# A row softmax: the scheduled kernel rewritten as one critical section with its own semaphores, the exponentials as loops with register addresses

**Chip, cores, metric.** One core of one Trainium2 chip. The metric is the time of one execution in microseconds (us) on the device, measured repeatedly. The profile's span, from the first recorded instruction to the last, is 1.8 us shorter than the measured time in nearly every run here.

## The reference

```python
def reference(x):                       # x: 16 x 1024 x 512 float32
    x_scaled = x / 0.5
    x_max = np.max(x_scaled, axis=-1, keepdims=True)
    exp_x = np.exp(x_scaled - x_max)
    return exp_x / np.sum(exp_x, axis=-1, keepdims=True)
```

That is 16384 rows of 512 numbers; 33.55 MB are read and 33.55 MB written.

## The kernel before

The rows form eight chunks of 128 partitions x 16 rows x 512 (4.19 MB). Six chunk buffers are used in rotation. Chunks are cut into eleven blocks: 4, 4, 8 rows of the first chunk, six whole chunks, 8 and 8 rows of the last. VectorE takes the negated maxima of a block (`shift`), ScalarE the exponentials with their row sums, VectorE the reciprocals and most of the product, and ScalarE one eighth of the product. The queue engine SyncE issues loads, ScalarE stores. Scheduling is manual, but the framework sets the semaphores.

```python
    def shift(i):                                   # VectorE
        ...
        nc.vector.tensor_reduce(negmax[:, 0:b], chunks[c][:, lo:hi, :], axis=AX, op=MAX, negate=True)
        nc.vector.tensor_scalar_mul(biases[i][:, 0:b], negmax[:, 0:b], 2.0)

    def exponentials(i):                            # ScalarE, unrolled
        ...
        for g in range(hi - lo):
            row = chunks[c][:, lo + g, :]
            nc.scalar.activation(out=row, in_=row, func=EXP, bias=biases[i][:, g : g + 1],
                                 scale=2.0, accum_out=sums[i][:, g : g + 1])

    def scale_vector(i):                            # VectorE: reciprocal, then product over 7/8 of the rows
        ...
    def scale_scalar(i):                            # ScalarE: the remaining eighth
        ...
    def store(i):                                   # one store per chunk, on ScalarE's queue
        ...
    shift(0); shift(1); exponentials(0)
    for i in range(n):
        if i + 1 < n:
            exponentials(i + 1)
        scale_vector(i)
        scale_scalar(i)
        if i + 2 < n:
            shift(i + 2)
        store(i)
```

(Cuts are marked with `...`.)

Of the kernel before, what the change touches and what calls it, by code (L numbers as in the profile page):

```python
# [1 line left out]

# [4 lines left out]


@with_exitstack
def kernel(  # L10
    ctx: ExitStack,
    tc: tile.TileContext,
    x: bass.AP,
    out: bass.AP,
):
    nc = tc.nc
    fp32 = mybir.dt.float32
    P = nc.NUM_PARTITIONS
    AX = mybir.AxisListType.X
    EXP = mybir.ActivationFunctionType.Exp  # L20
    COPY = mybir.ActivationFunctionType.Copy
    MAX = mybir.AluOpType.max

    D = x.shape[-1]
    xf = x.flatten_outer_dims()
    of = out.flatten_outer_dims()
    N = xf.shape[0]




    G = 16
    C = N // (P * G)
    assert C * P * G == N
    xr = xf.rearrange("(c p g) d -> c p g d", p=P, g=G)
    outr = of.rearrange("(c p g) d -> c p g d", p=P, g=G)
    WHOLE = [(0, G)]
    LOADS = [[(0, 4), (4, G)]] + [WHOLE] * 7
    BLOCKS = [[(0, 4), (4, 8), (8, G)]] + [WHOLE] * 6 + [[(0, 8), (8, G)]]
    STORES = [WHOLE] * 8  # L40
    BMAX = 16
    BUFS = 6

    data = ctx.enter_context(tc.tile_pool(name="data", bufs=BUFS))
    stats = ctx.enter_context(tc.tile_pool(name="stats", bufs=6))

    ctx.enter_context(tc.manual_schedule())


    warm = stats.tile([P, 1], fp32, name="warm", bufs=1)  # L50
    nc.vector.memset(warm, 0.0)  # L51
    nc.scalar.activation(out=warm, in_=warm, func=EXP)  # L52

    chunks = {}
    blocks = [(c, lo, hi) for c in range(C) for lo, hi in BLOCKS[c]]
    n = len(blocks)
    biases, sums, recips = {}, {}, {}

    def load(c):
        if c < BUFS:  # L60
            chunks[c] = data.tile([P, G, D], fp32, name="xt")
        else:
            chunks[c] = chunks[c - BUFS]
        xt = chunks[c]
        for lo, hi in LOADS[c]:
            nc.sync.dma_start(out=xt[:, lo:hi, :], in_=xr[c][:, lo:hi, :])  # L66

    def shift(i):
        c, lo, hi = blocks[i]
        if c not in chunks:  # L70
            load(c)
        b = hi - lo
        negmax = stats.tile([P, BMAX], fp32, name="negmax")
        nc.vector.tensor_reduce(  # L74
            negmax[:, 0:b], chunks[c][:, lo:hi, :], axis=AX, op=MAX, negate=True
        )
        biases[i] = stats.tile([P, BMAX], fp32, name="bias")
        nc.vector.tensor_scalar_mul(biases[i][:, 0:b], negmax[:, 0:b], 2.0)  # L78

    def exponentials(i):  # L80
        c, lo, hi = blocks[i]
        sums[i] = stats.tile([P, BMAX], fp32, name="sums")
        for g in range(hi - lo):
            row = chunks[c][:, lo + g, :]
            nc.scalar.activation(  # L85
                out=row,
                in_=row,
                func=EXP,
                bias=biases[i][:, g : g + 1],
                scale=2.0,  # L90
                accum_out=sums[i][:, g : g + 1],
            )


    def scale_vector(i):
        c, lo, hi = blocks[i]
        b = hi - lo
        k = b - b // 8
        recips[i] = stats.tile([P, BMAX], fp32, name="recip")
        nc.vector.reciprocal(recips[i][:, 0:b], sums[i][:, 0:b])  # L100
        rows = chunks[c][:, lo : lo + k, :]
        nc.vector.tensor_mul(  # L102
            rows, rows, recips[i][:, 0:k].unsqueeze(2).broadcast_to((P, k, D))
        )

    def scale_scalar(i):
        c, lo, hi = blocks[i]
        b = hi - lo
        for g in range(b - b // 8, b):
            row = chunks[c][:, lo + g, :]  # L110
            nc.scalar.activation(  # L111
                out=row, in_=row, func=COPY, scale=recips[i][:, g : g + 1]
            )

    def store(i):
        c, _, end = blocks[i]
        for lo, hi in STORES[c]:
            if hi == end:
                nc.scalar.dma_start(
                    out=outr[c][:, lo:hi, :], in_=chunks[c][:, lo:hi, :]  # L120
                )

    shift(0)
    shift(1)
    exponentials(0)
# [5 lines that stand above are left out]
        if i + 2 < n:  # L131
            shift(i + 2)
        store(i)


# [1 line left out]
_INS = ['x']  # L137
_OUTS = [((16, 1024, 512), 'float32')]


# [23 lines left out]
```

## Time and profile before

| | kernel before |
|---|---|
| time | 162.44 us median of 4 runs (162.20 to 162.51) |
| span of the profile | 160.57 us |
| transfers | the two data queues are busy 97.7% of the span |
| VectorE / ScalarE busy | 84% / 64% |
| first load issued / last store issued | 0.73 / 147.55 us |
| span's end after the last landing's wait | 0.80 us |

Read it from the bottom of the dependency: the two data queues carry all 67.1 MB and fill the sixteen DMA engines for 97.7% of the span, so their share of busy time decides first. VectorE's 84% comes second, and its place in the chain is what makes it matter. ScalarE is idle for the other 36%, and 41.2 us of that, 26% of the span, ended when a bias came from VectorE. The lines themselves stand in the prediction.

### The profile page before, as it was taken

What the parts mean: (1) busy time and instruction counts of PE and PEld (TensorE: products, weight loads), DVE (VectorE), ACT (ScalarE), POOL (GpSimd) and SP (SyncE); (2) the same over time, 40 slices, a digit from 0 to 9 for tenths busy, and PEclk for the clock granted to TensorE, in tenths of its full rate; (3) what the DMA queues carried; (4) which work ended last, traced back from release to release, by engine and by line L of the source; (5) the groups of instructions that cost most, each with busy time, mean ns of one, the idle gap of its engine ahead of it and who ended that gap; (6) DMA issues with size and microseconds to landing.
All of it is one profiled execution on the core that took longest, in us unless ns stands there. A gap on an engine that the chain in (4) does not pass through costs nothing.

```text
span 160.6 us, 402 instructions
## 1 busy us (share of the span) xinstructions
DVE 134.6 (84%) x45; ACT 102.1 (64%) x273; POOL 0.2 (0%) x4
## 2 busy tenths in 40 slices
DVE  0507999999999999999999999999999999957000
ACT  3071549069979963998199909991899891790000
POOL 0000000000000000000000000000000000000000
DMA  5999999999999999999999999999999999999993
GB/s 182 471 400 506 400 400 498 408 392 484 424 400 384 400 457 449 400 441 465 400 424 473 408 408 492 400 392 498 416 392 490 424 392 457 457 392 449 465 392 139
DMA packets 2450, 67.13 MB, mean 418 GB/s; under 512 B 272, under 2 KB 272, under 8 KB 272
## 3 DMA queue, kind: packets, MB, share of 16 engines
q1 hardware_dynamic: 1296, 33.56, 49.3%
q10 hardware_dynamic: 1152, 33.55, 48.4%
q14 instruction: 2, 0.02, 0.0%
HBM read 33.55 MB, written 33.55 MB: 418 GB/s over the span
## 4 chain that ended last, share of the span: by engine, by line
DVE 80%; DMA 7%; ACT 4%; issue 0%; SPq 0%
DVE negmax L74 42%; DVE xt L102 36%; DMA xt<-in_x_dram 7%; ACT xt L85 4%; DVE bias L78 1%; DVE recip L100 1%; SPq L66 0%
## 5 line engine op out<-in xcount | busy, mean ns | idle before, releaser
L85 ACT ACTIVATE xt<-xt,bias 128x512 f32<-128x512 f32 x128 | 90.4, 708 | 41.7 <-DVE bias L78 41.2
L74 DVE TENSOR_REDUCE negmax<-xt 128x16 f32<-128x8192 f32 (+2 forms) x11 | 69.9, 6352 | 9.5 <-DMA xt<-in_x_dram 9.5
L102 DVE TENSOR_TENSOR xt<-xt,recip 128x7168 f32<-128x7168 f32 (+2 forms) x11 | 62.0, 5637 | 0.4
L85 ACT ACTIVATION_READ_ACCUMULATOR xt<-xt,bias 128x1 f32 x128 | 23.9, 187 | 0.0
L111 ACT ACTIVATE xt<-xt,recip 128x512 f32<-128x512 f32 x15 | 9.9, 706 | 0.0
L100 DVE RECIPROCAL recip<-sums 128x16 f32<-128x16 f32 (+2 forms) x11 | 2.4, 218 | 1.8 <-ACT xt L85 1.8
L78 DVE TENSOR_SCALAR bias<-negmax 128x16 f32<-128x16 f32 (+2 forms) x11 | 1.9, 173 | 0.4
L52 ACT ACT_TABLE_LOAD x1 | 1.3, 1283 | 0.7 <-PEq L148 0.7
L51 DVE MEMSET warm<- 128x1 f32 x1 | 0.1, 59 | 0.8 <-PEq L148 0.8
L52 ACT ACTIVATE warm<-warm 128x1 f32<-128x1 f32 x1 | 0.2, 203 | 0.0
L148 POOL MEMSET const-bfloat16-1.0<- 128x1 bf16 x1 | 0.1, 103 | 0.0
L148 POOL MEMSET const-uint8-127<- 128x1 uint8 x1 | 0.1, 103 | 0.0
L148 POOL MEMSET const-float32-1.0<- 128x1 f32 x1 | 0.1, 100 | 0.0
L148 POOL MEMSET const-float32-0.0<- 128x1 f32 x1 | 0.1, 99 | 0.2 <-issue 0.2
## 6 DMA issues: line engine op xcount, KB each, us to landing
out_dram<-xt ACTq DMA_DIRECT2D x8, 4096.0 KB, 22.8
xt<-in_x_dram SPq DMA_DIRECT2D x7, 4096.0 KB, 30.2
xt<-in_x_dram SPq DMA_DIRECT2D x1, 3072.0 KB, 11.7
xt<-in_x_dram SPq DMA_DIRECT2D x1, 1024.0 KB, 4.9
```

Of the source, the lines that this page charges most:

```text
L51: nc.vector.memset(warm, 0.0)
L52: nc.scalar.activation(out=warm, in_=warm, func=EXP)
L74: nc.vector.tensor_reduce(negmax[:, 0:b], chunks[c][:, lo:hi, :], axis=AX, op=MAX, negate=True)
L78: nc.vector.tensor_scalar_mul(biases[i][:, 0:b], negmax[:, 0:b], 2.0)
L85: nc.scalar.activation(out=row, in_=row, func=EXP, bias=biases[i][:, g : g + 1], scale=2.0, accum_out=sums[i][:, g : g + 1],)
L100: nc.vector.reciprocal(recips[i][:, 0:b], sums[i][:, 0:b])
L102: nc.vector.tensor_mul(rows, rows, recips[i][:, 0:k].unsqueeze(2).broadcast_to((P, k, D)))
L111: nc.scalar.activation(out=row, in_=row, func=COPY, scale=recips[i][:, g : g + 1])
L148: nc = _bacc.Bacc("TRN2", target_bir_lowering=False, num_devices=1)
```

## The change

Its intent: no scheduler bookkeeping, one counting semaphore per engine plus one for each transfer, and a short instruction stream on ScalarE, as a block's exponentials become a loop whose row, bias and sum addresses are computed in registers. (A semaphore is a counter that one engine raises and another waits for; the profile lists what an engine's sequencer does, such as branches, register operations and DMA issues, with a q behind the engine's name, as ACTq, and the engine's own work without it.) What is computed, the order on each engine, the transfers and the six chunk buffers are the same; the small tiles of maxima, biases and sums become one tile of each kind. The diff, cut to its core:

```diff
-    ctx.enter_context(tc.manual_schedule())
+    ctx.enter_context(tc.tile_critical(no_gpsimd_drain=True))
+    vector_done = tc.alloc_semaphore("vector_done")
+    scalar_done = tc.alloc_semaphore("scalar_done")
+    loaded = {(c, hi): tc.alloc_semaphore(...) ...}          # one per load
+    stored = [tc.alloc_semaphore(f"stored_{c}") for c in range(C)]
...
+        vector(lambda: nc.vector.wait_ge(vector_done, done), False)   # between maximum and bias
...
     def exponentials(i):
         c, lo, hi = blocks[i]
-        for g in range(hi - lo):
-            row = chunks[c][:, lo + g, :]
-            nc.scalar.activation(out=row, in_=row, func=EXP, bias=..., accum_out=...)
+        scalar(lambda: nc.scalar.wait_ge(vector_done, need), 0)
+        summed[i] = scalar(lambda: exponential_loop(c, lo, hi), hi - lo)
+    def exponential_loop(c, lo, hi):
+        with nc.scalar.Fori(lo, hi) as g:
+            exponential(c, bass.ds(g, 1)).then_inc(scalar_done, 1)
...
+        scalar(lambda: nc.scalar.wait_ge(vector_done, scaled[i]), 0)  # ahead of a store
+        scalar(lambda: nc.scalar.wait_ge(scalar_done, need), 0)
...
+    for c in range(C - BUFS, C):
+        sync(lambda c=c: nc.sync.wait_ge(stored[c], 16))              # ahead of the section's end
```

## The prediction

The forecast's sum came to 0 + 0 + 0.25 + 0.2 + 0.3 = 0.75 us on 162.41, 163.2 us. What no trace or run of this case shows is cut from the text, with the cuts marked: figures for single steps of the sequencer and for the bandwidth; the terms worked out from them (the sequencer's time for a row of the loop, which was to add 0 us, the time to enter a loop, from which the 0.25 us came, and the cost of waits that are not merged); and the checks that followed from the entry.

> **What bounds the kernel now.** I read the page first: busy shares, the slices, the DMA queues.
>
> ```profile
> DVE 134.6 (84%) x45; ACT 102.1 (64%) x273; POOL 0.2 (0%) x4
> DMA  5999999999999999999999999999999999999993
> q1 hardware_dynamic: 1296, 33.56, 49.3%
> q10 hardware_dynamic: 1152, 33.55, 48.4%
> HBM read 33.55 MB, written 33.55 MB: 418 GB/s over the span
> ```
>
> The two queues together fill 97.7% of the sixteen engines' span. What is missing is 2.3% of 160.6 us, 3.7 us, and the slices put it into the first and the last slice. So the transfers leave no hole anywhere between, and no compute saving can take out more than the two ends hold.
>
> Then the chain of waits and, in the groups, VectorE's own idle time:
>
> ```profile
> by line: DVE negmax L74 41.7%; DVE xt L102 36.2%; DMA xt<-in_x_dram 7.3%; ACT xt L85 3.6%; DVE bias L78 1.1%; DVE recip L100 0.9%; issue 0.4%; SPq L66 0.2%
> ...
> 137.36 0.18 DVE bias L78
> 137.54 0.02 issue
> 137.56 5.76 ACT xt L85 x16
> 143.33 0.02 issue
> 143.35 0.21 DVE recip L100
> 143.56 0.02 issue
> 143.59 3.89 DVE xt L102
> ```
>
> From the second load's landing at 12.86 us VectorE runs without a pause to 147.48, except once: in the last block its reciprocal waits 1.8 us for ScalarE's exponentials. That is the only place where ScalarE lies on the chain. The chain ends 13 us before the span, since the last store is not one of its pieces.
>
> Does that store's issue time matter, with the transfers full? I compared the two lines' times to landing:
>
> ```profile
> DMA to landing us min/median/max: 12.2/22.8/32.4
> ...
> DMA to landing us min/median/max: 4.9/26.3/71.8
> ```
>
> The first answer is for the stores, the second for the loads. The shortest store is the last one: issued at 147.55, 4.19 MB. The shortest load is the first, 1.05 MB into empty queues. [...] So the last store waited for nobody: the store ahead was finished just as its own packets were ready to start. Transfers and VectorE's chain end in a tie. I call the slack of the last store's issue 0 to 0.3 us: earlier gains nothing, later costs the whole delay.
>
> Last, ScalarE's line (exponentials, then the idle time of their first row):
>
> ```profile
> L85 ACT ACTIVATE xt<-xt,bias 128x512 f32<-128x512 f32 x128 | 90.4, 708 | 41.7 <-DVE bias L78 41.2
> L85 ACT ACTIVATION_READ_ACCUMULATOR xt<-xt,bias 128x1 f32 x128 | 23.9, 187 | 0.0
> 79.62 0.72 ACT L85 ACTIVATE xt<-xt,bias 128x512 f32<-128x512 f32 x1 [4.00 <-DVE bias L78]
> ```
>
> The reads of the accumulator overlap the next exponential: in the timeline rows start 0.705 us apart. In a steady block sixteen rows take 63.01 to 74.31, two copies last to 75.63, the store is issued at 75.65 for 0.34 us, and the next block's bias comes 3.6 us later. The block's period is VectorE's: 8.61 + 0.17 + 0.17 + 7.63 and three gaps of 0.02, 16.6 us.
>
> [...] The trace of before has no branch in its body. [...]
>
> **The change part by part.** Loads, stores, sizes, buffers, blocks, and the order of instructions on every engine stay. So do both large VectorE operations (8677 and 7624 ns), hence the 16.6 us period.
>
> *Scheduler's waits replaced by own semaphores.* In the trace a dependent VectorE instruction starts 0.02 us after the one it waits for. There is nothing to gain. I expect the explicit waits to be merged into the instruction behind them, so 0 us. [...]
>
> *Unrolled exponentials become a loop.* 128 pairs of ACTIVATE and accumulator read become eleven loops. ScalarE's engine work is unchanged, 0.705 us a row. New is the sequencer's work per row. My estimate: three addresses (row, bias, sum) need about five register operations, the counter one[...]. Under 0.705 us, so the sequencer runs ahead and rows still start 0.705 us apart. [...]the number of register operations is a guess.
>
> *Entering a loop.* The wait for the bias now stands ahead of a loop[...]; then come a move, a branch and the first row's addresses before the first ACTIVATE[...]. In ten blocks this lies in ScalarE's 3.6 us of waiting and costs nothing. In the last block it goes onto the chain[...]. Less the slack of 0 to 0.3 us: +0.25 us.
>
> *The section's ends.* Entering and leaving a critical section may bring a drain and a barrier more. The existing entry barrier lasts to 0.7 us, and the end takes 0.8 us from the last landing (147.55 + 12.2 = 159.75) to the span's end. I put +0.2 us ahead of the first load, which shifts everything because loads start the chain and the transfers are full, and +0.3 us after the last store.
>
> Sum: 0 + 0 + 0.25 + 0.2 + 0.3 = 0.75 us on 162.41, 163.2 us.
>
> **The rivals.** *The loop is slower than the engine.* Let a row take s in the sequencer. Between 0.705 and about 0.90 us only the last block shows it: eight rows, up to 8 x 0.2 = 1.6 us, total about 164.7. [...] Beyond that ScalarE becomes the bound: at s = 1.1 us each steady block grows by 16 x 0.2 = 3.2 us; with about seven blocks of sixteen rows that is 22 us, about 185. For it: three register addresses per row[...]. [...] I give the first form two chances in ten, the second one in ten.
>
> *Own waits are costlier on VectorE.* [...] For it: VectorE has no slack on its chain. Against it: waits on the instruction itself are what the present 0.02 us gaps look like.
>
> *It gets faster.* For it: fewer instructions, fewer fetches, no scheduler bookkeeping; the first load could go out ahead of the 0.7 us barrier. Against it: the transfers are full from about 2 us to 159 us, so all there is to win is part of that 0.7 us: 161.9 at best. Two per cent, 3.2 us, is not there. In the same way a delay of earlier stores is hidden: the store issued at 133.08 lands 17.0 us later, 7 us more than its bytes need.
>
> **Range and chances.** The central sum is 163.2. Below, a free entry and merged waits give 162.2. Above, the mild form of the slow loop or unmerged waits give 164 to 165.5. Slower by over 2% means above 165.7: the strong loop rival with one chance in ten, and the sum of mild ones with a few more in a hundred. Faster by 2% needs fewer bytes.
>
> **What would show it.** In the changed profile the queues' shares should again add up to 97% or more, with the middle slices full. Product and reduction on VectorE should keep 7624 and 8677 ns, and gaps of 0.02 to 0.1 us between. Starts of exponentials inside a loop should stay 0.705 us apart; if larger, s is read there directly. [...] A first load issued much later than 0.73 us, VectorE waiting for exponentials in every block, or a DMA slice below 9 in the middle would make the prediction wrong.

## The result, and the profile after

The changed kernel takes 163.00 us (median of 4 runs, 162.65 to 163.19) against 162.44 us. The ratio is 1.0035, interval 1.0015 to 1.0055. Ratios here are the mean time of one kernel's fast runs over that of the other's of the same rounds, so not quite the ratio of the medians quoted. It is slightly slower, clear of noise, and well within 2%.

The page of the changed kernel, same lines as in the prediction:

```profile
DVE 134.6 (83%) x45; ACT 102.4 (63%) x273; POOL 0.2 (0%) x4
DMA  4999999999999999999999999999999999999991
q1 hardware_dynamic: 1296, 33.56, 49.1%
q10 hardware_dynamic: 1152, 33.55, 48.2%
```

The queues fill 97.3% of a span that is 0.84 us longer. Multiplied out they are as busy as before (156.9 and 157.1 us), and the middle slices stay full. Only the first and the last digit fell. So I looked for the added time at the two ends.

The start. These are the first seven loads on the queue engine's timeline, start and length; first the kernel before, then the changed one:

```profile
0.73 3.50 SPq L66 DMA_DIRECT2D xt<-in_x_dram  x7
```

```profile
0.94 3.51 SPq L86 DMA_DIRECT2D xt<-in_x_dram  x7
```

The first load goes out 0.21 us later: two more instructions, an empty one of the section's line L56 and a branch, now stand ahead of it on its engine.

The end. Here are instructions of the queue engine, with number, durations in ns (min/median/max), then first and last start in us; first the kernel before:

```profile
L159 SPq DRAIN  x3: 7/7/7, 159.8 to 160.1; - x3
```

Then the changed kernel, where L96 is the last wait for a store, L56 the section and L231 the final barrier:

```profile
L96 SPq EVENT_SEMAPHORE  x3: 17/28/28, 140.6 to 160.1; - x3
...
L56 SPq EVENT_SEMAPHORE  x2: 17/22/27, 160.3 to 160.5; - x2
...
L56 SPq DRAIN  x1: 7/7/7, 160.4 to 160.4; - x1
...
L231 SPq DRAIN  x3: 7/7/7, 160.6 to 160.9; - x3
```

The final barrier stands in the trace as drains and semaphore instructions on all engines. Before, it begins 0.07 us after the wait for the last store, which the trace has at 159.77, and the span ends 0.80 us after that wait. Afterwards the wait stands at 160.07; a branch, two semaphore instructions, a drain and an empty instruction come first, the barrier begins at 160.59, and the span ends at 161.41, 1.35 us after the wait. The end of the section costs 0.55 us: 0.46 ahead of the barrier, and a barrier that is 0.09 longer. These figures repeat: 0.80 in both traces without a section, 1.34 to 1.35 in six with one, with loops and without.

The loop, in the last block. These are pieces of the changed kernel's chain of waits (start, length, what; ACTq is ScalarE's sequencer):

```profile
137.45 0.18 DVE bias L119
137.65 0.03 ACTq L136
...
137.71 0.07 ACTq L136
...
138.18 0.07 ACTq L136
...
139.11 0.07 ACTq L136
...
141.38 2.32 ACT xt L126 x7
143.72 0.21 DVE recip L151
143.95 3.89 DVE xt L156
```

The pieces of 0.07 us are the first register operation of rows one, two and four (row three's is not among the pieces that the view lists): 0.47 us apart, 0.93 over the skipped row. That is the sequencer's time for one row while it runs ahead of the engine. The first exponential on the timeline:

```profile
137.92 0.72 ACT L126 ACTIVATE xt<-xt,bias  x1 [4.34 <-DVE recip L151]
```

It starts 0.30 us after the bias is done (137.62), against 0.03 us before (137.53 and 137.56). The bracket names the reciprocal, but the bias is what the loop waits for: the loop's own entry lies between (its move starts at 137.65, 0.03 us after the bias), and the listing takes whatever ended last. VectorE's wait for these exponentials, in the list of waits of the kernel before and of the changed one:

```profile
DVE recip L100 <- ACT xt L85: 1.8, 1, 1.8
```

```profile
DVE recip L151 <- ACT xt L126: 2.1, 1, 2.1
```

So it grew from 1.79 to 2.06 us, by the loop's entry (a move and two register operations, 0.27 us more than before), and the last store was issued at 147.88, 0.33 us later than before. Is that delay part of the added time? The experiments were made for this question.

### The profile page after: what moved, and what is told of

The parts are those of the page before. It is cut to its first block, busy times and chain, and to the rows that moved or that the text cites. A ratio compares the mean times of both kernels' runs of the same rounds, so it can differ in the third digit from the quotient of the medians.

```text
span 161.4 us, 921 instructions
## 1 busy us (share of the span) xinstructions
DVE 134.6 (83%) x45; ACT 102.4 (63%) x273; POOL 0.2 (0%) x4
## 4 chain that ended last, share of the span: by engine, by line
DVE 80%; DMA 7%; ACT 2%; issue 2%; ACTq 1%; SPq 0%
DVE negmax L113 41%; DVE xt L156 36%; DMA xt<-in_x_dram 7%; ACT xt L126 2%; DVE bias L119 1%; DVE recip L151 1%; ACTq L136 1%; SPq L86 0%; ACTq L126 0%; SPq L231 0%; SPq L56 0%
## 5 line engine op out<-in xcount | busy, mean ns | idle before, releaser
L126 ACT ACTIVATE xt<-xt,bias x128 | 90.6, 710 | 41.6 <-DVE recip L151 34.7
L126 ACT ACTIVATION_READ_ACCUMULATOR xt<-xt,bias x128 | 24.2, 189 | 0.0
## 6 DMA issues: line engine op xcount, KB each, us to landing
xt<-in_x_dram SPq DMA_DIRECT2D x1, 3072.0 KB, 11.6
```

The source lines that it names most:

```text
L126: return nc.scalar.activation(out=row, in_=row, func=EXP, bias=bias[:, c, g], scale=2.0, accum_out=sums[:, c, g],)
```

## The experiments

Twelve runs, all with correct output; one repeats the change and one the unrolled kernel. Medians of the kernel before: 162.26 us with the first four, 162.24 with the next four, 162.31 with the last four.

**All loops unrolled; and the last one alone.** The section and its semaphores stay.

```diff
-        with nc.scalar.Fori(lo, hi) as g:
-            exponential(c, bass.ds(g, 1)).then_inc(scalar_done, 1)
+        for g in range(lo, hi):
+            exponential(c, slice(g, g + 1)).then_inc(scalar_done, 1)
```

> The critical section and its semaphores stay, every loop is unrolled. My theory (what the change adds is one loop entry of about 0.3 us in the last block, plus about 0.1 to 0.2 us at the section's start and 0.5 us at its end; rows inside a loop cost nothing): about 0.25 us below the change, 162.75, with the last store issued near 147.6 and the end still 1.3 us after its landing. Rival A (the section and its semaphores cost nothing, the loop all of it): equal to the kernel before, 162.44. Rival B (all of it is the section; the last store's issue has slack): equal to the change, 163.0.

Measured: 163.22 us (162.87 to 163.89), ratio 1.0068 (1.0051 to 1.0086).

```diff
+        if (c, hi) == (C - 1, G):          # the last block only
+            for g in range(lo, hi):
+                exponential(c, slice(g, g + 1)).then_inc(scalar_done, 1)
+            return
         with nc.scalar.Fori(lo, hi) as g:
```

> Only the loop of the last block, eight rows, is unrolled; ten loops stay. My theory: the same time as with all loops unrolled within 0.1 us, 162.75, since the ten other loop entries lie in time in which ScalarE waits anyway. Rival (each loop costs a little somewhere): no gain over the change, 163.0, although the all-unrolled kernel gains.

Measured: 163.03 us, ratio 1.0040 (1.0027 to 1.0053). The last store in the first and in the second of these kernels:

```profile
147.64 0.34 ACTq L178 DMA_DIRECT2D out_dram<-xt  x1
```

```profile
147.56 0.34 ACTq L182 DMA_DIRECT2D out_dram<-xt  x1
```

It was issued as early as in the kernel before (147.55), and VectorE's last wait was 1.79 us again. Neither kernel ended earlier than the change. My expectation of a gain of 0.25 us fell, and rival B held: the entry of the last loop is on VectorE's chain and still costs nothing at the end. This contradicts the prediction's slack of 0 to 0.3 us for the last store.

**How much slack the last store has.** The store later:

```diff
+        for _ in range(16 if c == C - 1 else 0):
+            scalar(lambda: nc.scalar.sem_inc(idle, 1), 0)     # nobody waits for idle
         scalar(lambda: nc.scalar.dma_start(out=outr[c], ...
```

> The change, with sixteen idle semaphore increments (about 0.07 us each, 1.1 us) ahead of the issue of the last store. The two unrolled kernels issued it 0.2 to 0.3 us earlier than the change and ended no earlier; so the slack that I had put at 0 to 0.3 us must be larger. New theory: the last store's packets queue behind the store ahead, with about 0.65 us of slack counted from the kernel before (issue to last packet 11.8 us there, 11.1 in the kernel with slow rows); the change has used 0.33 of it, so 1.1 us more costs about 0.8: 163.8. Rival (no slack, my prediction): 164.1. Rival (slack over 1.5 us): 163.0.

Measured: 163.27 us, ratio 1.0062 (1.0049 to 1.0074). The last store and its time to landing (last number, us), in the kernel before, in the change and then here:

```profile
147.55 0.34 ACTq L119 DMA_DIRECT2D out_dram<-xt  x1
...
out_dram<-xt ACTq DMA_DIRECT2D x1, 4096.0 KB, 12.2
```

```profile
147.88 0.34 ACTq L178 DMA_DIRECT2D out_dram<-xt  x1
...
out_dram<-xt ACTq DMA_DIRECT2D x1, 4096.0 KB, 12.2
```

```profile
148.91 0.34 ACTq L181 DMA_DIRECT2D out_dram<-xt  x1
...
out_dram<-xt ACTq DMA_DIRECT2D x1, 4096.0 KB, 11.1
```

It was issued 1.03 us later than in the change and took 1.04 us less to land. The profiled span did not grow at all (161.40 against 161.41 us), and the time rose by 0.2 us over the change's 163.06 (repeat below), by 0.4 if the two ratios are compared. The 163.8 that I expected was missed: even my revised 0.65 us was too small. The slack in the kernel before is about 1.1 us, since its last store needed 12.2 us and a store of this size lands in 11.1 when nothing is ahead of it. (The two kernels with slow rows of 196.58 and 167.81 us below show that: there the store ahead had landed 2.4 and 1.0 us before the last was issued, and the last took 11.1 us.) The kernel before and the change stay inside this slack; the store here has used it up.

The store earlier, in the change and then in the kernel before:

```diff
-    BLOCKS = [[(0, 4), (4, 8), (8, G)]] + [WHOLE] * (C - 2) + [[(0, 8), (8, G)]]
+    BLOCKS = [[(0, 4), (4, 8), (8, G)]] + [WHOLE] * (C - 2) + [[(0, 12), (12, G)]]
```

> The change, with the last chunk's blocks of 12 and 4 rows instead of 8 and 8. The last block then has four exponentials, VectorE does not wait for them, and the last store is issued 1.5 to 2 us earlier. Theory (the transfers set the end): no gain, 162.9 to 163.1, the store's time to landing grows by what it was earlier. Rival (VectorE's chain sets the end): 161 to 161.5.

Measured: 163.12 us, ratio 1.0044 (1.0030 to 1.0058).

```profile
146.14 0.34 ACTq L178 DMA_DIRECT2D out_dram<-xt  x1
...
out_dram<-xt ACTq DMA_DIRECT2D x1, 4096.0 KB, 13.8
```

Issued 1.74 us earlier, it takes 1.7 us longer to land. VectorE no longer waits for exponentials in the last block at all, and the time stays.

> The kernel before, with the last chunk's blocks of 12 and 4 rows: the last store goes out 1.5 us earlier, and neither the section nor the loop is there. It is the best candidate that the runs so far suggest. Theory (transfers set the end): 162.2 to 162.5, the same as the kernel before. Rival (VectorE's chain sets it): 161.

Measured: 162.20 us, ratio 0.9990 (0.9976 to 1.0005). Its median is the only one below both kernels', but it can't be told from the kernel before. The transfers set the end: in twelve of the fourteen traces the last store lands 9.6 to 9.7 us after the store ahead of it, whether it was issued 4.2 us (the change with the early store) or 1.5 us (with the late one) before that store's landing. 4.19 MB in 9.65 us are 435 GB/s. The other two traces are those in which the store ahead had landed already.

**What a delay at the start costs.**

```diff
+    for _ in range(16):
+        sync(lambda: nc.sync.sem_inc(idle, 1))
     for c in range(C):                       # the loads
```

> The change, with sixteen idle increments on the queue engine ahead of the first load, which is issued 0.7 to 1.1 us later. Theory (transfers full from the first packet to the last): the whole delay is paid, 163.7 to 164.1; so the section's entry, 0.2 us, is paid whole too. Rival (the start has slack): 163.0.

Measured: 164.04 us, ratio 1.0116 (1.0090 to 1.0142). One run took 165.19 us, which I can't explain. The first load was issued at 1.93 instead of 0.94 us, 0.99 us later, the profiled span grew by 0.91, and the median is 1.0 us above the change. A delay of this size ahead of the first load is paid nearly whole. I take it that the 0.21 us of the section's entry are paid too; alone they are too small to show, since two profiles of the same unrolled kernel differ by 0.3 us.

**A second section.**

```diff
+    with tc.tile_critical(no_gpsimd_drain=True):
+        nc.vector.memset(extra, 0.0)
     ctx.enter_context(tc.tile_critical(no_gpsimd_drain=True))
```

> The change, with a second critical section of one tiny fill ahead of it. Theory (a section costs about 0.2 us at its start and 0.45 us at its end, from what stands between the last landing's wait and the final barrier in the two traces): the first load is issued 0.6 to 0.8 us later than in the change and all of it is paid, 163.6 to 163.8. Rival (a section is free, the added time is the loop's or chance): 163.0 to 163.1.

Measured: 164.25 us, ratio 1.0115 (1.0099 to 1.0131). The first load came at 1.65 us, 0.71 later, as expected, but the time lies 0.45 us above the expected range: it is 1.2 us above the change's, of which the load explains 0.7. The profiled span grew by 0.85 us. Of the rest, some 0.2 us lie outside the span (1.99 us between time and span instead of 1.78); what takes them stays open. A section's two ends cost 0.7 us when they stand together ahead of the loads. In the change they stand at the two ends: 0.21 + 0.55 = 0.76 us.

**The change and the unrolled section again**, in the same rounds. The kernels are unaltered.

> The change itself once more, beside the all-unrolled kernel on the same chip and in the same rounds, since they ran on different chips. Theory (the loop adds nothing, all of it is the section's two ends): 0.6 to 0.8 us over the kernel before, the same as the unrolled one within 0.15.

> The all-unrolled critical section once more. Theory: as the change in the same rounds within 0.15 us. Rival A (unrolling is slower by 0.2 to 0.3, as the first comparison hinted): 0.2 to 0.3 above it. Rival B (the loop's entry is paid): 0.25 below it.

Measured: 163.06 us, ratio 1.0038 (1.0023 to 1.0054), for the change, and 163.05 us, ratio 1.0046 (1.0024 to 1.0068), unrolled. They are the same, on one chip and in the same rounds, and so the loop adds nothing that these runs can show. The first hint that unrolling is slower comes from single runs of 163.65 to 163.89 us, of which the unrolled kernel had three in twelve and the change none in ten; I have no profile of such a run and leave it open.

**Slower rows.** Does the loop cost nothing because the sequencer's 0.47 us lie under the engine's 0.705?

```diff
             exponential(c, bass.ds(g, 1)).then_inc(scalar_done, 1)
+            for _ in range(5):               # 10 in the second kernel
+                nc.scalar.sem_inc(idle, 1)
```

> Five semaphore increments that nobody waits for are added behind each row of the loop, some 0.3 us of sequencer work, so a row takes about 0.75 to 0.8 us there instead of 0.47. My theory: starts of exponentials move from 0.705 to that figure, but only the last block's eight rows reach the end: +0.3 to +0.8 us on the change, 163.3 to 163.8, VectorE's wait for exponentials in the last block growing by the same. Rival (row time counts in every block): 80 rows or more times 0.07, 168 us or more.

Measured: 165.33 us, ratio 1.0191 (1.0176 to 1.0206), 1.5 us above my upper figure. Rows took 0.805 us where they ran as intended, so an increment costs (0.805 - 0.47) / 5 = 0.067 us. VectorE's reciprocals that had to wait, on its timeline (start, length, in brackets the idle time before):

```profile
47.17 0.25 DVE L154 RECIPROCAL recip<-sums 128x16 f32<-128x16 f32 x1 [0.75 <-ACT xt L127]
...
64.06 0.25 DVE L154 RECIPROCAL recip<-sums 128x16 f32<-128x16 f32 x1 [0.17 <-ACT xt L127]
...
127.09 0.25 DVE L154 RECIPROCAL recip<-sums 128x16 f32<-128x16 f32 x1 [0.73 <-ACT xt L127]
...
146.31 0.20 DVE L154 RECIPROCAL recip<-sums 128x8 f32<-128x8 f32 x1 [2.75 <-ACT xt L127]
```

They add up to 4.40 us against 2.06 in the change, 2.34 more; the median rose by 2.3 us, the profiled span by 2.04. That the two agree doesn't show that every wait is paid: the last store was issued 2.59 us later and landed 2.05 us later, 11.6 us after its issue, so it still had 0.5 us of slack. The last wait grew by 0.69 us, seven steps of 0.098, as expected. What I had overlooked are the two sixteen-row blocks next to half blocks, the first and the third line that wait 0.75 and 0.73 us. While ScalarE works on them, VectorE has only 3.89 + 8.61 us or 7.63 + 4.34 us of its own work with the small operations, 12.8 and 12.3 us instead of 16.6. Their rows are 0.829 us apart in the first (the fourth loop) and 0.795 in the other (the ninth), so sixteen take 13.3 and 12.7 us, and the loop's entry comes on top. The threshold that I computed for the steady block does not hold for these two.

The 0.17 us belong to the fifth loop, in which something else shows. ScalarE's timeline in the fifth and in the seventh loop:

```profile
48.53 0.72 ACT L127 ACTIVATE xt<-xt,bias  x1 [0.78 <-ACT xt L168]
...
49.78 0.72 ACT L127 ACTIVATE xt<-xt,bias  x1 [0.43 <-issue]
...
50.75 0.72 ACT L127 ACTIVATE xt<-xt,bias  x1 [0.15 <-issue]
...
51.71 0.72 ACT L127 ACTIVATE xt<-xt,bias  x1
```

```profile
81.07 0.72 ACT L127 ACTIVATE xt<-xt,bias  x1 [0.96 <-DVE recip L154]
...
81.88 0.72 ACT L127 ACTIVATE xt<-xt,bias  x1
...
82.69 0.72 ACT L127 ACTIVATE xt<-xt,bias  x1
```

Rows are 0.805 us apart in the seventh loop, as intended, and 0.96 in the fifth (after 1.25 in its first step). The change has such a loop as well: in its seventh, here and in the repeat, the sequencer's rows are 0.63 us apart instead of 0.47, which still fits under 0.705; only one row there comes 0.2 us late.

> Ten such increments, a row of about 1.05 to 1.1 us. My theory: beyond 0.90 us a row ScalarE becomes the bound: its sixteen-row block takes about 19 to 19.7 us instead of 16.6, VectorE waits for exponentials in every block, total 183 to 191 us, and the transfers show holes. Rival (the transfers keep the time): under 170 us.

Measured: 196.58 us, ratio 1.2113 (two runs), above my range. Rows are 1.142 us apart, more than I had intended, and in two of the loops 1.37 and 1.35 on average. The waits and, below, the slices of this kernel:

```profile
ACT xt L127 <- issue: 43.5, 117, 0.8
DVE recip L154 <- ACT xt L127: 36.2, 7, 8.8
```

```profile
DMA  5999999999999959999699989900990079597595
```

Now ScalarE waits for its own sequencer ("issue") at nearly every row, VectorE waits for ScalarE in seven blocks, and the transfers have holes. ScalarE's block lasts 20.07 us (77.00 to 97.07) instead of 16.6. The rival of the prediction exists: at 0.805 us a row the steady blocks were still free (the seventh loop's first row above waited 0.96 us for VectorE), at 1.14 they are not.

**The slow loop moved.** In the change and in both kernels with slower rows, the loops with clearly longer steps were those during which a packet on the instruction queue was fetched (at 84.8 us in the change's seventh; at 54.4 in the fifth above; at 37.7 and 162.6 in the fourth and the tenth, the two slow ones of the last kernel).

```diff
     scalar(lambda: nc.scalar.activation(out=warm, in_=warm, func=EXP))
+    for _ in range(8):
+        scalar(lambda: nc.scalar.sem_inc(idle, 1), 0)
```

> The kernel with slow rows (165.33, rows 0.805 us apart, but 0.978 in the fifth loop), with eight idle increments ahead of the first loop, where ScalarE waits for the first load anyway. In that kernel, in the change and in the slower one, the one or two loops whose rows are slower are those during which an instruction packet was fetched. Theory[...]: [...]no loop is slow and the time falls by 0.8 to 1.6 us, to about 164. Rival (something at that time slows the sequencer, the transfers for instance): the fifth loop stays at 0.978, 165.3.

Measured: 167.81 us, ratio 1.0322 (1.0289 to 1.0354). The time was missed, and in the wrong direction; I had also put too much of the lost time down to the fifth loop. The theory that can be tested was that a loop is slow by its place in the instruction stream, and that eight instructions ahead take the fifth loop off it, to 0.805 us a row. This held. All eleven loops now run at 0.795 to 0.815 us a row, the fifth at 0.806: eight instructions ahead of the first loop took the slowness out of it. So it seems to belong to where the loop lies in the instruction stream, not to what happens at that time; this rests on one trace of each kernel. What makes a place slow is not shown. The issue of stores in this kernel (count, ns min/median/max):

```profile
L183 ACTq DMA_DIRECT2D out_dram<-xt x8: 338/338/5952, 47.9 to 153.5; - x8
```

One issue took 5952 ns instead of 338; it held ScalarE from 47.9 to 53.9 us, and the instruction packet came at 52.2, inside it. VectorE then waited 3.45 us for the fifth loop, which started late. Whether the issue waited for this packet is not shown; nor does the profile say for which engine a packet was.

## Why the prediction was right

The median of 163.0 us lies 0.2 us below the predicted 163.2. That transfers bound the kernel and that the section's two ends are paid was right; that the sum came out so close, 0.76 for 0.75 us, is luck, since two of its terms were wrong by the same amount. Term by term, in the prediction's own steps:

- *Own semaphores on VectorE, 0 us*: right. From the second maximum (12.97 against 12.88 us) to the last bias (137.45 against 137.36) VectorE runs 0.09 us later throughout; the gaps between dependent instructions stayed at 0.02 us.
- *A row of the loop, hidden under 0.705 in the sequencer*: right; 0.47 measured. The number of register instructions for the addresses was guessed wrong, two (fused ones of 73 and 52 ns in most rows) instead of five. With one more of 35 ns and a compare-and-branch of 45 ns the records of a row add up to 0.21 us; the rest of the 0.47 us lies between them. That it is hidden is shown by the unrolled kernel of the same rounds (163.05 against 163.06), and that it would not be hidden if slower by the kernels with 0.805 and 1.142 us a row. The rival's first form was incomplete: between 0.705 and 0.90 us not only the last block shows it, but also the two whole blocks next to half blocks.
- *Loop entry, 0.25 us at the end*: the entry is 0.27 us more than before (no branch stands in it) and does delay the last store (0.33 us), but it costs nothing. The failed step is the sentence that the last store "waited for nobody". I had compared the times to landing of the first load and of the last store, less the time of their bytes, as if what is left were the same thing: at the 435 GB/s measured above, 4.9 - 2.4 = 2.5 and 12.2 - 9.6 = 2.6 us, an estimate. A store of this size alone needs 11.1 us, so the one at 12.2 had waited about 1.1 us. The slack was about 1.1 us, not 0 to 0.3.
- *Ends of the section, 0.2 and 0.3 us*: the first was 0.21, and paid as far as the late first load can show. The second was 0.55, the term that was too small. Too much for the loop and too little for the exit nearly cancelled: 0.21 + 0.55 = 0.76 us, against 0.56 and 0.75 us between the medians of two sets of runs (0.57 and 0.62 by the ratios). The new layout of the small tiles was not tested alone; the operations kept their times (8.61 and 7.63 us on VectorE, 708 and 710 ns for an exponential).
- *"Faster" rival*: right that the transfers leave nothing. There were fewer instruction packets, one for two in the traces of the change and of the kernel before. Even the last store issued 1.4 us earlier in the kernel before changed the time by no more than noise.

Where did the gain that was hoped for go? There was none to be had. The loop and the semaphores change work that lies beneath the transfers, and only the section's two ends stick out.

## What to carry to other kernels

When the transfers are full from end to end (97.7% of the span here), a rewrite of waits and instruction streams can pay little except at the two ends; look first at when the first load is issued and what stands between the last landing and the final barrier, because a delay ahead of the first load was paid nearly whole here (0.91 us of span for 0.99). A register loop on ScalarE cost nothing here, with a sequencer time per row of 0.47 us under the engine's 0.705, but measure the slack at the blocks with the shortest period, and look at the rows of all loops, since one was a third slower (0.63 for 0.47 us) apparently by where it lay in the instruction stream. Judge a late issue by making it later, not by subtracting another transfer's fixed cost.
